# A hybrid trunk layer on one core: values between the r blocks, inverse and values in four tiles, wide triples between product bursts, and the next group's key norms and half of its sigmoids in the solve

## The chip, the core and the metric

The kernel runs on one core of a Trainium2 chip. The metric is device time in microseconds (us): the median of three runs. One more execution is profiled, and all durations of single instructions come from it. TensorE (PE) multiplies, VectorE (DVE), ScalarE (ACT) and GpSimd (POOL) work on tiles, SyncE (SP) issues transfers. Each engine works its own instructions off in the order in which the program has them and waits where an operand or a buffer isn't ready.

## The reference

One layer of a causal decoder trunk on a sequence of 1024 tokens and 1024 channels. From the normalised input, one projection gives the inputs of three branches (pooling, RWKV-7, attention to 256 memory tokens) and three gates; the branches are projected, gated and added, and a feed-forward part with a short causal convolution follows. The change lies in the RWKV-7 branch, which has 16 heads of 64 channels:

```python
zr = z_rwkv + (token_shift(z_rwkv) - z_rwkv) * mu_shift
r, k, v, dw, da, dg = jnp.split(zr, ...)
w_log = -softplus(-(w0 + tanh(dw) @ w_up_decay)) - 0.5
a = sigmoid(a0 + da @ w_up_a)
kk = k * k_k;  kk = kk * rsqrt(sum(kk * kk) + L2_EPS)      # per head: the key norm
k_eff = k * (1 + (a - 1) * k_a)
# per token t, state of 64 x 64 per head:
sa = state @ (-kk);  state = state * decay + sa (kk * a)^T + v k_eff^T;  y = state @ r
y = layer_norm(y) * ln_x_w + ln_x_b + sum(r * k_eff * r_k) * v
```

The decay is exp(-exp(w_log)), so it needs one sigmoid of w0 + ..., and a needs one of a0 + ....

## The kernel before, in words

Inputs, weights and results stay in fp32. A projection is made of *wide triples*: `mm3` (line 177) splits both factors in two fp32r parts and issues three matmuls of 128x128 by 128x512 (lines 180 to 182); each is called a wide below. Eight triples make one tile of 128 output columns by 512 tokens, so a column block has 16 triples. The two parts of a weight are made by ACT (`whi`, line 132) and POOL (`wlo`, line 139) ahead of use.

The recurrence is done in chunks of 64 tokens. `rwkv_group` (line 475) handles four groups g = 0 to 3 of four heads, as two column blocks i = 0, 1. Its parts, in program order:

- *norms and sigmoids*: `lengths` (sums of squares with the matmul `phd`, then Ln and Exp), a table load of ACT, and for each block the small matmuls `psu` (lines 502 and 503) with the sigmoids w0 (into `tBN`) and a0 (into `tHV`); the weights come by `load_up2` (line 379), which POOL splits. Then a second table load (line 208).
- *preparation* (lines 521 to 554): a scan of the decays, two Exp, the r block (48 wides, `in_block`, with a token shift on ACT, line 329, and DVE, lines 331 to 335), and copies and products that make `AR` (left factors, with r times decay at line 553) and `BK` (right factors; ACT's copies of lines 544, 549 and 550).
- *values* (lines 571 to 581): the matmul `pv` transposes v, ACT copies it to `HV`, and it is stored.
- *products* (lines 589 to 610): for each block four bursts of matmuls `ps` of 64 rows. Each burst fills two banks of four (`product_bank`), ACT copies half to `RB` and DVE multiplies half with a mask into `NT` and `AR` (lines 606 to 610). `RB` is multiplied with a mask (line 612).
- *bonus* `pbo` (line 562), after block 0, and the transposes `pt` (line 630) of `BK`.
- *solve* (lines 645 to 657): DVE inverts 32x32 triangles by forward substitution, then `place` copies the results (line 664).
- *inverse* (lines 667 to 682): `pz` and `pw` join the 32x32 parts to the inverse of 64x64 triangles, with DVE and ACT copying in between; then `NT` is stored.

A fill keeps PE at work in the solve: `group_kv` makes the next group's k and v blocks, and `fill_to(n)` (line 881) issues triples of other branches' projections until n have been issued in all: 48 more per group ahead of pz, and 256 in all ahead of the last pz. After the fourth group `chain` (line 732) runs the recurrence over the chunks, with the rest of the fill between its matmuls; its first matmul is `pr`.

`later(i, j)` only says that instruction i must stand after j, and a scheduler puts the instructions of each engine in an order that fits all of these. `PE.matmul` in fp32 shows as two records in the profile where both factors are fp32.

## Time and profile before

| what | us |
|---|---|
| median of 3 runs | 1940.28 (1934.13 to 1942.58) |
| the profiled execution | 1933.07 |
| its span | 1931.4 |
| mean granted clock of PE | 0.994 |
| DVE busy, ACT busy, POOL busy | 1366.2, 1048.7, 785.7 |

A busy time is the sum of an engine's instructions on the slowest core. In the timeline views a row has the start, the duration, the engine, the line and operation, the output and inputs with their shape, and the count of records drawn together; brackets hold the idle time ahead and what ended it. PEclk is the clock that the throttle granted to PE, as a share of full speed. The windows view gives each engine's busy time and the count of instructions in a stretch.

### The profile page before, as it was taken

What the parts mean: (1) busy time and instruction counts of PE and PEld (TensorE: products, weight loads), DVE (VectorE), ACT (ScalarE), POOL (GpSimd) and SP (SyncE); (2) the same over time, 40 slices, a digit from 0 to 9 for tenths busy, and PEclk for the clock granted to TensorE, in tenths of its full rate; (3) what the DMA queues carried; (4) which work ended last, traced back from release to release, by engine and by line L of the source; (5) the groups of instructions that cost most, each with busy time, mean ns of one, the idle gap of its engine ahead of it and who ended that gap; (6) DMA issues with size and microseconds to landing.
All of it is one profiled execution on the core that took longest, in us unless ns stands there. A gap on an engine that the chain in (4) does not pass through costs nothing.

```text
span 1931.4 us, 33821 instructions
## 1 busy us (share of the span) xinstructions
PE 1869.7 (97%) x12204; PEld 1515.9 (78%) x12204; DVE 1366.2 (71%) x2054; ACT 1048.7 (54%) x2190; POOL 785.7 (41%) x867
## 2 busy tenths in 40 slices
PE   8999999998999999999999999999999999999997
PEld 6767877876777888788788888888788888888886
DVE  8677677677677446657964534679798888877798
ACT  6685385385484355555664345555454454544544
POOL 4422221222221211121323455566599888821441
PEclk9999999999999999999999999999999999999999
DMA  5326236326239669975246444653322222289775
GB/s 165 130 73 184 93 88 179 100 77 186 94 95 303 207 195 317 329 220 183 96 139 207 130 131 141 194 164 123 105 85 90 86 80 85 88 263 211 170 189 144
DMA packets 269641, 296.28 MB, mean 153 GB/s; under 512 B 18336, under 2 KB 219168, under 8 KB 266400
## 3 DMA queue, kind: packets, MB, share of 16 engines
q1 hardware_dynamic: 248480, 271.56, 44.5%
q0 software_dynamic: 11856, 14.16, 4.5%
q10 hardware_dynamic: 9136, 8.39, 1.5%
q8 instruction: 96, 1.57, 0.3%
q14 instruction: 73, 0.60, 0.1%
HBM read 207.00 MB, written 87.03 MB: 152 GB/s over the span
## 4 chain that ended last, share of the span: by engine, by line
PE 65%; DVE 5%; DMA 3%; ACT 1%; issue 1%; POOL 0%; SPq 0%; DVEq 0%; ACTq 0%; POOLq 0%
PE psg L180 11%; PE psg L182 11%; PE psg L181 11%; PE psf L182 6%; PE psf L180 6%; PE psf L181 6%; PE psd L181 3%; PE psd L182 3%; PE psd L180 3%; PE py L780 1%; DMA R<-d_f 1%; PE pr L780 1%; PE ph L780 1%; DMA hv<-d_hv 1%; DMA gt<-d_bv 1%
## 5 line engine op out<-in xcount | busy, mean ns | idle before, releaser
L139 POOL TENSOR_TENSOR wlo<-wraw,whi 128x256 fp32r<-128x256 f32 x464 | 403.9, 883 | 827.1 <-ACT whi L132 772.8
L180 PE MATMUL psg<-hh,whi 128*128 128x512 f32 x928 | 373.9, 403 | 12.7 <-ACT whi L132 8.5
L182 PE MATMUL psg<-hh,wlo 128*128 128x512 f32 x928 | 368.7, 398 | 1.6 <-POOL wlo L139 1.4
L181 PE MATMUL psg<-hl,whi 128*128 128x512 f32 x928 | 369.0, 398 | 0.3 <-DVE hl L266 0.2
L132 ACT CAST whi<-wraw 128x256 fp32r<-128x256 f32 x472 | 181.5, 403 | 246.1 <-PE psg L181 96.1
L180 PEld LDWEIGHTS psg<-hh,whi 128*128 128x128 f32 x928 | 175.7, 189 | 55.8 <-ACT whi L132 14.4
L182 PEld LDWEIGHTS psg<-hh,wlo 128*128 128x128 f32 x928 | 176.0, 190 | 42.6 <-POOL wlo L139 4.9
L181 PEld LDWEIGHTS psg<-hl,whi 128*128 128x128 f32 x928 | 176.0, 190 | 36.7 <-issue 1.4
L1192 POOL TENSOR_TENSOR wt<-a,wt 128x256 fp32r<-128x256 f32 x136 | 155.5, 1167 | 35.3 <-ACT wt L1191 35.3
L181 PE MATMUL psd<-f,u 128*128 128x512 f32 x292 | 114.0, 390 | 0.5 <-DVE f L1608 0.4
L180 PE MATMUL psd<-f,u 128*128 128x512 f32 x292 | 113.2, 391 | 1.2 <-ACT f L1604 1.2
L182 PE MATMUL psd<-f,u 128*128 128x512 f32 x292 | 113.7, 389 | 0.0
L182 PE MATMUL psf<-h2h,wt 128*128 128x512 f32 x272 | 105.9, 389 | 0.1
L180 PE MATMUL psf<-h2h,wt 128*128 128x512 f32 x272 | 105.9, 389 | 0.0
L181 PE MATMUL psf<-h2l,wt 128*128 128x512 f32 x272 | 105.8, 389 | 0.0
L1206 DVE SCALAR_TENSOR_TENSOR d<-z,pv,d 128x1023 f32<-128x1023 f32 x68 | 101.1, 1491 | 2.1
L1192 POOL TENSOR_TENSOR wt<-s,wt 128x256 fp32r<-128x256 f32 x68 | 81.2, 1213 | 2.8 <-ACT wt L1191 1.9
L181 PE MATMUL psf<-t,wt 128*128 128x512 f32 x204 | 79.4, 389 | 0.0
L180 PE MATMUL psf<-t,wt 128*128 128x512 f32 x204 | 79.4, 389 | 0.0
L182 PE MATMUL psf<-t,wt 128*128 128x512 f32 x204 | 79.4, 389 | 0.0
L1204 ACT ACTIVATE d<-z,pv 128x1024 f32<-128x1024 f32 x34 | 42.4, 1247 | 65.7 <-DVE z L1286 49.9
L1191 ACT CAST wt<-a 128x256 fp32r<-128x256 f32 x136 | 50.7, 404 | 40.8 <-POOL wt L1192 25.9
(436 smaller groups left out, 4499.2 us busy)
## 6 DMA issues: line engine op xcount, KB each, us to landing
wraw<-in_w_in SPq DMA_DIRECT2D x176, 128.0 KB, 2.4
a<-in_w_fup SPq DMA_DIRECT2D x128, 128.0 KB, 2.4
d_ar<-AR SPq DMA_DIRECT2D x24, 512.0 KB, 4.2
d_zg<-st SPq DMA_DIRECT2D x48, 256.0 KB, 3.5
ring<-d_ar SPq DMA_DIRECT2D x8, 1536.0 KB, 11.9
wraw<-in_w_fup SPq DMA_DIRECT2D x80, 128.0 KB, 2.5
fraw<-d_f SPq DMA_DIRECT2D x33, 256.0 KB, 4.1
d_rb<-RB SPq DMA_DIRECT2D x16, 512.0 KB, 5.7
```

The source lines that it names most:

```text
L132: i = A.copy(hi, src)
L139: (V if lo_on_dve[0] else G).tensor_tensor(lo, src, hi.bitcast(F32), op=ALU.subtract)
L180: first = PE.matmul(ps, wh, xh, start=start, stop=False)
L181: PE.matmul(ps, wh, xl, start=False, stop=False)
L182: last_mm[0] = PE.matmul(ps, wl, xh, start=False, stop=stop).ins
L780: m = PE.matmul(out_, l, r, **kw)
L1191: A.copy(w[0][:, us], src[u])
L1192: low = eng.tensor_tensor(w[1][:, us], src[u], w[0][:, us].bitcast(F32), op=ALU.subtract)
L1204: A.activation(d, z, AF.Identity, scale=col("cw2", j), bias=col("cb", j))
L1206: V.scalar_tensor_tensor(d[:, n:], z[:, :T - n], col(cw, j), d[:, n:], op0=ALU.mult, op1=ALU.add)
```

## The change

- The four w0 sigmoids of a group stay in front of the preparation. The norms, the a0 sigmoids, both `load_up2` (now with a tile `ulo2` each) and the table load ahead of them are issued for group g + 1 between `group_kv` and the solve's end of group g (`lengths(g + 1, nxt)`). Group 0 has them at its start as before.
- `fill_to` ahead of pz leaves 8 triples of each group's 48 undone (`LEFT`). `covered(n)` issues n of them, behind a given instruction, at new places: 6 ahead of the w0 sigmoids, 1 between those of block 1, and in both blocks 1, 2 and 2 triples ahead of the second, third and fourth burst. In group 0 one triple goes behind the norms. In group 3 triples also go between the bonus matmuls and the first four transposes. Ahead of pz 744, 1176, 1608 and 2064 wides have been issued in all, where it was 768, 1200, 1632 and 2064.
- `values` now stands between the two r blocks, in four tiles of 64x64 at a time, two banks for each block, with both blocks in one burst of 128 records. `HV` has the memory that `NT` takes later, where it had that of `tHV`.
- pz and pw are issued for both halves in one burst each, in four tiles of 32x32, with one pair of copies ahead of pw for each half.
- The bursts of a group are put in order one behind the other (`burst`), the scan runs over 256 tokens instead of 512, and phd's two matmuls change places.

The diff, cut to its core (of what is removed, most stands in the code above and isn't repeated):

```diff
 LAST = HK - 4
+GROUP, LEFT = 48, 8
+TAKEN = 4 * GROUP + 64
 PV = {}
...
+    last_up = [None]
+    def raised(u, e, l, t0, dst, bias):
+        ps = psg.tile([P, 512], F32, name="psu", tag="g0")
+        first = PE.matmul(ps, u[0][:, e], l[:, t0:t0 + 512], start=True, stop=False)
+        last_up[0] = PE.matmul(ps, u[1][:, e], l[:, t0:t0 + 512], start=False, stop=True).ins
+        act(dst, ps, AF.Sigmoid, bias=bias)
+        return first
+    def lengths(g, kv):
         sp = rw.tile([P, 2, 2, T], FR, name="sp", tag="AR")
         tHV = rw.tile([P, 2, 2, T], F32, name="tHV", tag="HV")
+        def norms():
             for i in range(2):
                 for s, ps in square_sums(kv[i][:, 0], col("k_k", 2 * g + i), tHV[:, i, 1], sp[:, i]):
                     rstd(tHV[:, i, 1, s], ps, 1)
         if g:
-            lengths()
+            norms()
             table(SIGMOID)
+        ups = [load_up2(w_upd[2 * g + i], i) for i in range(2)]
         for i in range(2):
             for t0, _ in HALVES:
+                raised(ups[i], 1, la, t0, tHV[:, i, 0, t0:t0 + 512], col("a0", 2 * g + i))
+        return tHV, ups, norms
+    def rwkv_group(g, kv, ready):
+        tagA, tagB, tagC = ([f"X{i}{(2 * g + n) % 3}" for i in range(2)] for n in range(3))
+        tBN = [rw.tile([P, 2, T], F32, name=f"tBN{i}", tag=tagC[i]) for i in range(2)]
+        tHV, ups, norms = lengths(g, kv) if g == 0 else ready
...
+        BKs = [rw.tile([P, NCH, P], F32, name=f"BK{i}", tag=tagB[i]) for i in range(2)]
+        cover, burst = [GROUP * g - LEFT if g else 0], [None]
+        def covered(n, behind=None):
+            cover[0] += n
+            fence[0] = behind
+            wide = fill_to(cover[0])
+            fence[0] = None
+            return wide
+        if g:
+            covered(6, placed[0])
+        last = None
+        for i in range(2):
+            for t0, _ in HALVES:
+                m = raised(ups[i], 0, ld, t0, tBN[i][:, 0, t0:t0 + 512], col("w0", 2 * g + i))
+                if g and i:
+                    later(m, covered(1, last))
+                last = last_up[0]
         table(LN_EXP)
         if g == 0:
-            lengths()
+            norms()
+            covered(1)
         AR = rw.tile([P, 2, 3, T], F32, name="AR", tag="AR")
-        vs = []
+        vs = [kv[i][:, 1] for i in range(2)]
         turn = [0]
...
             return pool.tile([P, 4, 2, C], F32, name=name, tag=tag)
+        def values():
+            lo, up = slice(0, 64), slice(64, 128)
+            HV = rw.tile([P, 2, NCH, C], F32, name="HV", tag="NT")
+            after = last_mm[0]
+            for i in range(2):
+                ps = [pool.tile([P, 8, C], F32, name="pv", tag=tag)
+                      for pool, tag in (((psk, "k"), (psc, "c")) if i else ((pss, "s"), (pss, "s")))]
+                for c in range(8):
+                    for n in (1, 0):
+                        t = slice((8 * n + c) * C, (8 * n + c + 1) * C)
+                        for rows, at_ in ((lo, lo if n else up), (up, up if n else lo)):
+                            m = PE.matmul(ps[n][at_, c], vs[i][rows, t], cent[rows], start=True, stop=True)
+                            later(m, after)
+                            after = m.ins
+                for n in range(2):
+                    A.copy(HV[up, i, 8 * n:8 * n + 8], ps[n][lo if n else up])
+                    A.copy(HV[lo, i, 8 * n:8 * n + 8], ps[n][up if n else lo])
+                spill(d_hv, (g, i), HV[:, i])
+            return HV
         for i in range(2):
...
-            for t0, _ in HALVES:
-                s = slice(t0, t0 + 512)
+            for t0 in range(0, T, 256):
+                s = slice(t0, t0 + 256)
                 V.tensor_tensor_scan(t2_[:, s], smask, t2_[:, s], 0.0, op0=ALU.mult, op1=ALU.add)
             act(t3_, t2_, AF.Exp, scale=-DECAY)
             act(t2_, t2_, AF.Exp, scale=DECAY)
             V.tensor_copy(Dc[:, p], c3(t3_)[:, :, C - 1])
             in_block(8 + p, shifted(p, r_))
+            if i == 0:
+                HV = values()
             dst = c3(AR[:, i, 0])
...
             V.tensor_tensor(r_, r_, t3_, op=ALU.mult)
-            vs.append(t1_)
-
         def bonus(i):
             t0_ = kv[i][:, 0]
             for t0, _ in HALVES:
                 s = slice(t0, t0 + 512)
                 ps = pss.tile([P, 512], F32, name="pbo", tag="s")
-                PE.matmul(ps, bones, t0_[:, s], start=True, stop=True)
+                m = PE.matmul(ps, bones, t0_[:, s], start=True, stop=True)
+                if g == 3 and (i or t0):
+                    later(m, covered(1, burst[0]))
+                burst[0] = m.ins
                 V.tensor_tensor(t0_[:, s], vs[i][:, s], ps, op=ALU.mult)
...
                 ps = [product_bank("ps1"), product_bank("ps2")]
-                m = None
+                after = covered(min(2, c0 // 4), burst[0]) if c0 else None
                 for c in range(4):
                     t = slice((c0 + c) * C, (c0 + c + 1) * C)
                     for e, rows in ((1, up), (0, lo)):
+                        m = PE.matmul(ps[e][:, c], BK[i][rows, c0 + c], AR[rows, i, e:e + 2, t],
+                                      start=True, stop=True)
+                        if after is not None:
+                            later(m, after)
+                        after = m.ins
+                burst[0] = after
                 A.copy(RB[i][:, 0, cs], ps[0][:, :, 1])
...
                 for c in range(4):
-                    PE.transpose(ps[:, c], BK[i][:, c0 + c], ident)
+                    m = PE.transpose(ps[:, c], BK[i][:, c0 + c], ident)
+                    if c == i == 0 and g == 3:
+                        later(m, covered(1, burst[0]))
+                burst[0] = m.ins
                 A.copy(BKN[i][:, c0:c0 + 4], ps)
...
         nxt = group_kv(g + 1, []) if g < 3 else None
+        ready = lengths(g + 1, nxt) if g < 3 else None
         tb1 = rw.tile([P, 2, 32, 32], F32, name="tb1", tag=tagB[1])
...
         V.transpose(X.rearrange("p u t -> p t u"), S)
-        fill_to(48 * (g + 1))
+        fill_to(GROUP * (g + 1) - (LEFT if g < 3 else 0))
         if g == 3:
             w_queue[0] = A
-            fill_to(256, solve)
+            fill_to(TAKEN, solve)
         for us in (slice(0, NCH), slice(NCH, 2 * NCH)):
             for q, (qs, bs) in enumerate(quads):
                 place = V.tensor_copy(NTu[qs, us, bs], X[qs, us]).ins
+        placed[0] = place
         Z = tmp
         ends = [(slice(e, e + 32), slice(e + 32, e + 64)) for e in (0, 64)]
+        us = slice(0, 16), slice(16, 32)
+        ps = pss.tile([P, 16, 32], F32, name="pz", tag="s")
+        for u in range(16):
+            for h in range(2):
+                for ends_ in ends:
+                    m = PE.matmul(ps[ends_[1 - h], u], NTu[ends_[0], 16 * h + u, 32:64],
+                                  S11[ends_[0], 16 * h + u], start=True, stop=True)
+                    if u == h == 0:
                         later(m, place)
+        for h in range(2):
+            moved = [A.copy(Z[32:64, us[h]], ps[ends[0][1 - h]]),
+                     V.tensor_copy(Z[96:128, us[h]], ps[ends[1][1 - h]])]
+        ps = pss.tile([P, 16, 32], F32, name="pw", tag="s")
+        for u in range(16):
+            for h in range(2):
+                for ends_ in ends:
+                    m = PE.matmul(ps[ends_[h], u], Z[ends_[1], 16 * h + u],
+                                  NTu[ends_[1], 16 * h + u, 32:64], start=True, stop=True)
+                    for i in moved:
+                        later(m, i.ins)
+        for h in range(2):
+            for ends_ in ends:
+                A.copy(NTu[ends_[0], us[h], 32:64], ps[ends_[h]])
         for i in range(2):
             spill(d_nt, (g, i), NT[:, i])
-        return nxt
+        return nxt, ready
     def spill(dst, at_, src):
...
     fill += [(34 + j, spilled(d_zg[j], col("gate_b", j))) for j in range(24)]
-    filled = []
+    filled, fence = [], [None]
     def fill_steps(j, evac, behind):
...
                     later(m, behind)
+                if fence[0] is not None:
+                    later(m, fence[0])
                 filled.append(last_mm[0])
...
         return filled[n - 1]
+    placed = [None]
     first_kv = start()
     for lo in (0, 64):
         s = slice(lo, lo + 64)
         V.tensor_scalar(cent[s], ident[s, lo:lo + 64], 1.0, -1.0 / 64, op0=ALU.mult, op1=ALU.add)
     kv = group_kv(0, [first_kv])
     hi_on_act[0] = True
+    ready = None
     for g in range(4):
-        kv = rwkv_group(g, kv)
-    chain(lambda v: 279 + 121 * (v - 1) // 46 if v else 262)
+        kv, ready = rwkv_group(g, kv, ready)
+    chain(lambda v: TAKEN + 23 + (377 - TAKEN) * (v - 1) // 46 if v else TAKEN + 6)
     covered = fill_to(416)
```

What the change does to three engines, as the second group's instructions stand. First ACT, from a BK copy of the preparation on; the numbers behind the names tell tiles apart, tBN0 and BK0 are those of block 0. Before:

```order
L544 COPY BK0_2337<-BK0_2337 64x16x64
L132 CAST whi_2540<-wraw_2539 128x256
L546 ACTIVATE tHV_2336<-tHV_2336,oka_137,pv_88 128x1024
L329 ACTIVATE AR_2419<-psg_2479,omu_135 128x512
L132 CAST whi_2546<-wraw_2545 128x256
L549 COPY BK0_2337<-tBN0_2334 64x16x64
L550 COPY BK0_2337<-tBN0_2334 64x16x64
L544 COPY BK1_2338<-BK1_2338 64x16x64
L132 CAST whi_3427<-wraw_3426 128x256
L549 COPY BK1_2338<-tBN1_2335 64x16x64
L329 ACTIVATE AR_2419<-psg_2551,omu_135 128x512
L550 COPY BK1_2338<-tBN1_2335 64x16x64
```

and now:

```order
L599 COPY BK1_2377<-BK1_2377 64x16x64
L566 COPY HV_2513<-pv_2514 64x512
L567 COPY HV_2513<-pv_2514 64x512
L566 COPY HV_2513<-pv_2515 64x512
L567 COPY HV_2513<-pv_2515 64x512
L604 COPY BK0_2376<-tBN0_2374 64x16x64
L566 COPY HV_2513<-pv_2553 64x512
L567 COPY HV_2513<-pv_2553 64x512
L566 COPY HV_2513<-pv_2554 64x512
L567 COPY HV_2513<-pv_2554 64x512
L605 COPY BK0_2376<-tBN0_2374 64x16x64
L601 ACTIVATE tHV_1944<-tHV_1944,oka_137,pv_88 128x1024
```

The copies of HV, which came behind all BK copies and four casts further on, now stand between the copies of block 0's BK, and block 1's activation (line 601 now) and copies come behind them.

DVE at the end of the preparation, where the shifted r (psg), the bonus factor (kv) and r times decay (AR from AR and tBN) are made and the first evacuations (NT and AR from ps) begin. Before:

```order
L552 SCALAR_TENSOR_TENSOR kv0_1549<-AR_2419,pv_88,tHV_2336 128x1024
L553 TENSOR_TENSOR AR_2419<-AR_2419,tBN0_2334 128x1024
L331 COPY zc_2526<-psg_2551 128x1
L335 SCALAR_TENSOR_TENSOR AR_2419<-psg_2551,pv_88,AR_2419 128x511
L333 SCALAR_TENSOR_TENSOR AR_2419<-zc_2526,pv_88,AR_2419 128x1
L335 SCALAR_TENSOR_TENSOR AR_2419<-psg_2579,pv_88,AR_2419 128x511
L552 SCALAR_TENSOR_TENSOR kv1_1712<-AR_2419,pv_88,tHV_2336 128x1024
L553 TENSOR_TENSOR AR_2419<-AR_2419,tBN1_2335 128x1024
L609 TENSOR_TENSOR NT_2620<-ps2_2705,mstrict_102 64x256
L606 TENSOR_TENSOR NT_2620<-ps1_2704,mstrict_102 64x256
L607 TENSOR_TENSOR AR_2419<-ps1_2704,mstrict_102 64x256
L610 TENSOR_TENSOR AR_2419<-ps2_2705,mstrict_102 64x256
```

and now:

```order
L607 SCALAR_TENSOR_TENSOR kv0_1617<-AR_2423,pv_88,tHV_1944 128x1024
L608 TENSOR_TENSOR AR_2423<-AR_2423,tBN0_2374 128x1024
L602 TENSOR_TENSOR tHV_1944<-tHV_1944,kv1_1780 128x1024
L603 TENSOR_TENSOR tBN1_2375<-tHV_1944,tBN1_2375 128x1024
L333 COPY zc_2613<-psg_2638 128x1
L337 SCALAR_TENSOR_TENSOR AR_2423<-psg_2638,pv_88,AR_2423 128x511
L335 SCALAR_TENSOR_TENSOR AR_2423<-zc_2613,pv_88,AR_2423 128x1
L337 SCALAR_TENSOR_TENSOR AR_2423<-psg_2666,pv_88,AR_2423 128x511
L607 SCALAR_TENSOR_TENSOR kv1_1780<-AR_2423,pv_88,tHV_1944 128x1024
L653 TENSOR_TENSOR NT_2707<-ps1_2712,mstrict_102 64x256
L608 TENSOR_TENSOR AR_2423<-AR_2423,tBN1_2375 128x1024
L654 TENSOR_TENSOR AR_2423<-ps1_2712,mstrict_102 64x256
```

Block 1's last product with tBN stood ahead of all evacuations; now the first evacuation of the first burst stands ahead of it and the others behind it.

PE from the middle of the first product burst of block 0 on (line 601 before, 646 now). Before, the second burst follows the first directly:

```order
L601 MATMUL ps2_2705<-AR_2419,BK0_2337 128x128
L601 MATMUL ps1_2704<-AR_2419,BK0_2337 128x128
L601 MATMUL ps2_2705<-AR_2419,BK0_2337 128x128
L601 MATMUL ps1_2704<-AR_2419,BK0_2337 128x128
L601 MATMUL ps2_2721<-AR_2419,BK0_2337 128x128
L601 MATMUL ps1_2720<-AR_2419,BK0_2337 128x128
L601 MATMUL ps2_2721<-AR_2419,BK0_2337 128x128
L601 MATMUL ps1_2720<-AR_2419,BK0_2337 128x128
```

and now a triple stands between them:

```order
L646 MATMUL ps2_2713<-AR_2423,BK0_2376 128x128
L646 MATMUL ps1_2712<-AR_2423,BK0_2376 128x128
L182 MATMUL psg_2754<-hh_146,whi_2731 128x512
L183 MATMUL psg_2754<-hl_147,whi_2731 128x512
L184 MATMUL psg_2754<-hh_146,wlo_2732 128x512
L646 MATMUL ps2_2729<-AR_2423,BK0_2376 128x128
L646 MATMUL ps1_2728<-AR_2423,BK0_2376 128x128
L646 MATMUL ps2_2729<-AR_2423,BK0_2376 128x128
```

The third and the fourth burst have two triples ahead of them, and the scheduler adds others where they fit.

More of the change, by code (lines that the diff above doesn't have):

```diff
@@ L98, in trunk_kernel @@
     mincl = const.tile([P, 64], F32, name="mincl")
-    smask = const.tile([P, 512], F32, name="smask")
+    smask = const.tile([P, 256], F32, name="smask")
     G.memset(mstrict, 1.0)
@@ L372, in load_up, with load_up2 @@
         return hi, lo
-    ulo2 = lr.tile([P, 2, P], FR, name="ulo2")
-    G.memset(ulo2.bitcast(F32), 0.0)
-    def load_up2(ap):
+    ulo2 = [lr.tile([P, 2, P], FR, name=f"ulo2{i}") for i in range(2)]
+    for t in ulo2:
+        G.memset(t.bitcast(F32), 0.0)
+    def load_up2(ap, i):
         raw, hi, _ = up_tiles()
-        lo = ulo2
+        lo = ulo2[i]
         SP.dma_start(raw, ap)
@@ L470, in square_sums @@
             ps = pss.tile([P, 512], F32, name="phd", tag="s")
[L471 to L472 removed]
+            PE.matmul(ps, bonesr, sp[:, 1, t0:t0 + 512], start=True, stop=False)
+            PE.matmul(ps, bonesr, sp[:, 0, t0:t0 + 512], start=False, stop=True)
             yield slice(t0, t0 + 512), ps
[L475 to L476 removed]
+    last_up = [None]
[6 more added lines that the diff above has]
+    def lengths(g, kv):
         sp = rw.tile([P, 2, 2, T], FR, name="sp", tag="AR")
[L478 removed]
         tHV = rw.tile([P, 2, 2, T], F32, name="tHV", tag="HV")
[L481 to L487 removed]
+        def norms():
             for i in range(2):
@@ L570, in rwkv_group @@
         NT = rw.tile([P, 2, NCH, C], F32, name="NT", tag="NT")
-        HV = rw.tile([P, 2, NCH, C], F32, name="HV", tag="HV")
-        for i in range(2):
-            for c0 in (0, 8):
-                ps = pss.tile([P, 8, C], F32, name="pv", tag="s")
-                for c in range(8):
-                    tsl = slice((c0 + c) * C, (c0 + c + 1) * C)
-                    PE.matmul(ps[64:128, c], vs[i][0:64, tsl], cent[0:64], start=True, stop=True)
-                    PE.matmul(ps[0:64, c], vs[i][64:128, tsl], cent[64:128], start=True, stop=True)
-                A.copy(HV[64:128, i, c0:c0 + 8], ps[64:128])
-                A.copy(HV[0:64, i, c0:c0 + 8], ps[0:64])
-            spill(d_hv, (g, i), HV[:, i])
         RB = [rw.tile([P, 2, NCH, C], F32, name=f"RB{i}", tag=tagC[i]) for i in range(2)]
@@ L600, in rwkv_group @@
                     for e, rows in ((1, up), (0, lo)):
-                        m, was = PE.matmul(ps[e][:, c], BK[i][rows, c0 + c], AR[rows, i, e:e + 2, t],
-                                           start=True, stop=True), m
-                        if was is not None:
-                            later(m, was.ins)
+                        m = PE.matmul(ps[e][:, c], BK[i][rows, c0 + c], AR[rows, i, e:e + 2, t],
[4 more added lines that the diff above has]
+                burst[0] = after
                 A.copy(RB[i][:, 0, cs], ps[0][:, :, 1])
```

36 lines of the change are left out of this document (3 added, 33 removed).

## The prediction

> **What bounds the kernel now.** The page comes first: the span, and how much of it each engine works.
> ```profile
> span 1931.4 us, 33821 instructions
> PE 1869.7 (97%) x12204; PEld 1515.9 (78%) x12204; DVE 1366.2 (71%) x2054; ACT 1048.7 (54%) x2190; POOL 785.7 (41%) x867
> ```
> PE works 97% of the span, so on average only fewer or shorter PE instructions help. The change touches the four head groups alone, so I cut that stretch into stages: the timeline of PE gives the points at which each group's inverse starts and the point at which the chain begins.
> ```profile
> 372.81 1.20 PE L672 MATMUL pz<-tb,NT 32*32 32x32 f32 x64
> 373.94 0.50 PE L502 MATMUL psu<-ld,uhi 128*128 128x512 f32 x1
> 655.84 1.20 PE L672 MATMUL pz<-tb,NT 32*32 32x32 f32 x64
> 665.63 0.56 PE L780 MATMUL pr<-hv,ring 64*64 64x64 f32 x12
> ```
> The first inverse starts at 231.30 (next fence), so a period takes 141.5 us (372.81 − 231.30, and half of 655.84 − 372.81). The 9.8 us up to the first pr are the tail. Now the second group in five stages, from its predecessor's pz on: preparation, products of block 0, bonus and transposes, products of block 1, solve.
> ```profile
> core 0: us, PE busy (x) PEld busy (x) DVE busy (x) ACT busy (x) POOL busy (x), PEclk, DMA share, GB/s
> 231.30:283.70 52.40, 51.57 (x560) 40.31 (x559) 32.16 (x34) 41.34 (x62) 12.35 (x12) 1.00 0.26 78
> 283.70:291.30 7.60, 5.29 (x67) 4.27 (x67) 5.15 (x13) 7.42 (x25) 0.00 (x0) 1.00 0.61 165
> 291.30:306.00 14.70, 14.41 (x61) 9.64 (x61) 8.18 (x14) 8.21 (x15) 2.21 (x3) 1.00 0.82 242
> 306.00:319.10 13.10, 10.71 (x94) 9.06 (x93) 9.46 (x19) 10.12 (x27) 0.72 (x1) 0.87 0.40 124
> 319.10:372.80 53.70, 52.87 (x232) 42.88 (x230) 46.63 (x94) 19.08 (x40) 19.61 (x26) 1.00 0.41 124
> ```
> In the preparation PE is busy 51.57 of 52.40 us, yet ACT already has 41.34 us of work there: a preparation much shorter than that finds ACT late. In both product stages PE idles over 2 us. In the solve PE is busy 52.87 of 53.70, and DVE, which does the solve, 46.63: some 7 us of DVE slack.
>
> The two product stages on PE's timeline, with the idle time ahead of a burst and its releaser:
> ```profile
> 283.73 2.08 PE L601 MATMUL ps<-AR,BK 64*128 64x128 f32 x32
> 287.65 1.16 PE L601 MATMUL ps<-AR,BK 64*128 64x128 f32 x16 [1.41 <-DVE AR L610]
> 289.41 1.16 PE L601 MATMUL ps<-AR,BK 64*128 64x128 f32 x16 [0.60 <-DVE AR L610]
> 291.33 0.67 PE L562 MATMUL pbo<-kv,bonesr 128*128 128x512 f32 x1 [0.33 <-DVE AR L610]
> 306.02 2.06 PE L601 MATMUL ps<-AR,BK 64*128 64x128 f32 x32
> 310.77 1.16 PE L601 MATMUL ps<-AR,BK 64*128 64x128 f32 x16 [1.79 <-ACT RB L605]
> 312.53 1.99 PE L601 MATMUL ps<-AR,BK 64*128 64x128 f32 x16 [0.60 <-ACT whi L132]
> 312.00:316.00 4.00, 3.47 (x22) 3.10 (x23) 3.51 (x7) 1.71 (x6) 0.72 (x1) 0.58 0.11 33
> ```
> A burst costs 1.0 (two in 2.08). The third and fourth wait until the evacuations of an earlier burst have freed a bank: 1.41 + 0.60 + 0.33 in block 0, 1.79 + 0.60 in block 1. After the latter the granted clock falls to 0.58 for 4.00 us, a loss of 0.42 × 4.00 = 1.7.
>
> **The change part by part.** The prices, from rows: wide steps, bursts in two and four tiles, and the edge between a burst and the wides.
> ```profile
> 400.19 0.39 PE L180 MATMUL psg<-hh,whi 128*128 128x512 f32 x1
> 400.64 0.39 PE L182 MATMUL psg<-hh,wlo 128*128 128x512 f32 x1
> 245.19 0.22 PE L577 MATMUL pv<-cent,kv 64*64 64x64 f32 x1
> 245.25 0.22 PE L577 MATMUL pv<-cent,kv 64*64 64x64 f32 x1
> 245.46 0.50 PE L181 MATMUL psg<-hl,whi 128*128 128x512 f32 x1
> 245.79 0.40 PE L182 MATMUL psg<-hh,wlo 128*128 128x512 f32 x1
> 678.54 0.69 PE L780 MATMUL pu<-Rs,pair 64*64 64x64 f32 x32
> 679.16 0.50 PE L180 MATMUL psg<-hh,whi 128*128 128x512 f32 x1
> ```
> A wide in a row costs 0.227 (0.45 for two). pv, in two tiles, issues two matmuls per 0.058. The chain's pu, in four tiles, starts 32 in 0.62; as 8 × 0.058 + 0.16 that is four per 0.058 and 0.16 ahead of the burst. The first wides behind a burst take 0.33 each (245.46 to 245.79), which is 0.10 more, twice: 0.21. An edge therefore costs 0.16 + 0.21 = 0.37.
>
> *Four tiles.* pz needs 1.13 for 64 matmuls (372.81 to 373.94); four such bursts of pz and pw make 4.5 per group. All 64 pairs in four tiles go in two bursts of 1.13, so 2.2 are saved. pv has 128 matmuls, 64 × 0.058 + 4 × 0.16 = 4.4; in four tiles 32 × 0.058 + 0.16 = 2.0, so 2.4 are saved. Whether 32-row tiles overlap as pu's do isn't in the trace: the gain per group lies between 0 and 4.6, and I take 4.6 because pu's tiles also share their rows in pairs. The Trainium skill, page “TensorE: Matmul & The Clock Gate”, section “The mechanism”, says that loading weights overlaps running matmuls only where the row group differs. Two of the four new tiles have the same rows, so by that rule this term is 0; pu's four per 0.058 speak against it.
>
> *Preparation on PE.* Ahead of block 0's first product now stand 120 wides (before, 144, and the norms and eight more sigmoid matmuls): 120 × 0.227 = 27.2, pz and pw 2.3, eight sigmoid matmuls 1.8, pv 2.0, six burst edges at 0.21 1.3: 34.6 instead of 52.4. Two bursts (2.0), ten wides (2.3) and two edges (0.7) later, at 39.6, PE reaches the third burst, which needs the first one's bank.
>
> *Preparation on ACT and DVE.* This is the chain that PE now meets:
> ```profile
> 254.36 1.28 ACT L208 ACT_TABLE_LOAD   x1
> 273.83 1.05 ACT L550 COPY BK<-tBN 64x1024 f32<-64x1024 f32 x1
> 274.90 1.02 ACT L132 CAST whi<-wraw 128x256 fp32r<-128x256 f32 x3
> 276.84 0.69 ACT L329 ACTIVATE AR<-psg,omu 128x512 f32<-128x512 f32 x1 [0.91 <-PE psg L182]
> 279.80 1.70 DVE L553 TENSOR_TENSOR AR<-AR,tBN 128x1024 f32<-128x1024 f32 x1
> 281.00 0.58 ACT L579 COPY HV<-pv 64x512 f32<-64x512 f32 x1
> 285.77 0.43 DVE L609 TENSOR_TENSOR NT<-ps,mstrict 64x256 f32<-64x256 f32 x1 [4.27 <-ACT RB L608]
> ```
> pz, ten wides, three edges and pw end at about 5.8. Then ACT makes four copies of 0.58 (8.1), the four w0 sigmoids (0.69 each, as a pass of that shape), a cast (0.34) and a store copy (0.58), 11.8, and the table load, 13.1. From the table's end (255.64) to the end of the last BK copy (274.88) ACT took 19.2 before; all that work stands there again. New in this queue are the eight HV copies (8 × 0.58 = 4.7), which stood behind the BK copies; they are taken in full, since ACT idles little there. Another 1.5 (between 0 and 2 copies of 1.05) are for the second block's BK copies, which now stand behind one another. Sum 38.5. Three casts (1.0) and, from the start of the r shift to the start of AR's product, 2.96 more: 42.5. That product (1.70) now stands among the evacuations of the first burst (4 × 0.43): its bank is free at about 46.0. Then PE waits 6.4, and I price the half clock after it at 1.7, as after the 1.79 wait.
>
> pbo then starts at 46.0 + 1.0 (third burst) + 1.7 (six wides and an edge) + 1.0 (fourth) + 1.7 (half clock) = 51.4 after pz, against 60.0 (291.33 − 231.30). **Gain 8.6.**
>
> *Bonus and transposes*: two wides fewer, gain 0.4.
>
> *Products of block 1*: eleven more wides stand between the bursts, 2.5, and two more edges, 0.7. The waits of 2.4 and the half clock of 1.7 can go for it, which would gain 0.9. But DVE still needs 1.7 for each burst and multiplies RB behind them, so I leave 0.7 of wait: gain 0.2, between −1.5 (the waits only move) and 0.9. The Trainium skill, the same page, section “Why this matters for your kernels”, names idle gaps of over about 3 us between bursts as what drops the clock. By that figure the half clock behind 1.79 and 0.60 has nothing to do with these waits, its 1.7 does not go with them, and the sum would be 4 × 1.7 = 6.8 lower; the row at 0.58 stands right behind them, so I keep the credit.
>
> *Solve*: 252 wide slots instead of 230, since the norms and half of the sigmoids moved in with fewer fill triples ahead: 22 × 0.227 = 5.0, and two edges, 0.8: loss 5.8. DVE's solve would start 78 after pz and need its 46.8; PE reaches the next pz only at 138, so PE sets that end and DVE keeps over 10 us. Norms and the weights' split on ACT, DVE and POOL are hidden there (19.08 and 19.61 of 53.70 busy). If that cover were gone, they would cost no more than the two table loads of 1.28. On SP the stores of HV stand ahead of one load of a fill block and the next group's first loads; these are due over 25 us later, so I cost that at nothing (a late load would cost up to its 2 to 3 us, once per group).
>
> Net for groups 2 and 3: 8.6 + 0.4 + 0.2 − 5.8 = 3.4 each. The fourth group takes the 24 wides that the first gave up and has triples between bonus and transposes too; its solve is filled up to 256 triples in both versions: I put it at 2.6. The tail gets nine fixed wides and two bursts fewer edges: 7.2 instead of 9.8, 2.6. The first group gives up 24 wides, but they go to the fourth, and PE stands longer at its first product, with the HV copies ahead of its casts: 1.5 (between −3 and 5). **Sum 3.4 × 2 + 2.6 + 2.6 + 1.5 = 13.5.** The profiled execution (1933.07, span 1931.4) would become 1919.6. It lies at the low end of the three runs (1934.13 to 1942.58), so against their median of 1940.28 I forecast **1927**.
>
> **The rivals.** *A, PE does not wait at the third burst.* ACT's queue has idle time that takes up the HV copies, and the bank is free when PE comes. For it: ACT idles 11 of the 52.4 us. Against: most of these are ahead of the table, not behind it. Then 6.4 + 1.7 more are gained in three groups and some 3 in the first: 13.5 + 24.3 + 3 = 41, **1900**.
>
> *B, the wait is about 10 us*, because casts for the second r block also stand behind the HV copies. The gain of 3.4 vanishes in each group and what is left is the tail: **1939**.
>
> *C, four tiles do not overlap*, by the rule on row groups above. All of 4 × 4.6 = 18 goes back: 1927 + 18 = **1945**. pu's row speaks against it.
>
> *D, slower.* In block 0 the chain on ACT's queue (four HV copies ahead of each of the first block's last two BK copies) gets longer than the wides in front of PE: the casts of the r block, queued behind copies that wait for pv, hold PE up, PE delays the shift, and the shift delays the evacuations. PE then waits in two places. Each us of it costs four, one in each group. Break-even is at a wait of 6.4 + 13.5/4 = 9.8; from about 12.2 (another 9.7 in four groups) on it is slower by over 0.5%, and at 14 it would be 1940.3 − 13.5 + 4 × 7.6 = **1957**. For it: ACT is busy 41.34 of 52.40 us already, and everything gained on PE ends in this chain. Against: the waits would have to double.
>
> **How the numbers follow.** Forecast 0.52, A 0.20, B 0.10, C 0.03, D 0.15. About 0.5% (9.7 us) is what a measurement of this kernel can tell from no change. The forecast's own range, with block 1 between −1.5 and 0.9 in four groups, the first group between −3 and 5, and the wait uncertain by 2, is 1918 to 1937; some two thirds of it are faster by over 0.5%. Faster: 0.34 + 0.20 (A) = 0.54. Same: 0.18 + 0.10 + 0.03 = 0.31. Slower: 0.15 (D). From 1900 to 1948 the range holds the forecast, B, C and the nearer part of A, and leaves out D.
>
> **What would show it.** Right: the period between two pz falls by 3 to 4 us, to about 138; pbo comes 51 us after pz; the third burst of block 0 shows a wait of 4 to 8 us released by DVE's evacuation, with a granted clock below 0.7 behind it; the solve is at 59 to 60 us with PE over 97% busy; pz and pw take 1.1 each. Wrong: no wait there (A); pv or pz at the old length (C); waits ahead of casts in the r blocks, or a period over 142 (D).

## The result, and the profile after

The changed kernel takes 1959.7 us, the median of 6 runs (1955.25 to 1961.28), against 1938.09 us of the kernel before (1933.61 to 1942.58, 6 runs): a ratio of 1.0108, with a 95% interval of 1.0086 to 1.0130. It is slower by about 1.1%, where 1927 was forecast.

The page of the profile after shows nearly the same work in a longer span. PE is busy 1865.0 us instead of 1869.7; the span has grown by 22.1.

```profile
span 1953.5 us, 33838 instructions
PE 1865.0 (95%) x12204; PEld 1505.5 (77%) x12204; DVE 1358.8 (70%) x2070; ACT 1049.2 (54%) x2190; POOL 784.1 (40%) x868
```

The same five stages of the second group, as windows of the trace after (from pz: preparation, products of block 0, bonus and transposes, products of block 1, solve; the columns are those of the windows before):

```profile
239.15:274.30 35.15, 34.93 (x513) 28.10 (x513) 23.16 (x27) 30.64 (x45) 9.07 (x8) 1.00 0.41 117
274.30:291.06 16.76, 10.24 (x81) 7.98 (x81) 11.08 (x20) 10.14 (x27) 4.59 (x5) 0.80 0.24 72
291.06:305.74 14.68, 14.29 (x62) 9.52 (x60) 7.38 (x12) 7.08 (x14) 0.73 (x1) 1.00 0.72 221
305.74:318.93 13.19, 12.52 (x105) 9.70 (x105) 9.01 (x19) 11.24 (x30) 3.04 (x3) 1.00 0.46 148
318.93:387.76 68.83, 60.97 (x255) 47.67 (x254) 49.18 (x100) 27.03 (x52) 20.84 (x27) 0.95 0.31 97
```

Against before, the stages differ by −17.25, +9.16, −0.02, +0.09 and +15.13 us, which is +7.1 for the period. The first four are within 0.6 us of the forecast's −17.8, +9.2, −0.4 and −0.2. The solve was forecast at +5.8 and came out at +15.1: PE is busy only 60.97 of 68.83 us there, where before it was busy 52.87 of 53.70.

PE stands idle for 15.7 us of this period (148.61 − 132.94), and two places on its timeline hold 12.2 of them. The first is the third burst of block 0:

```profile
285.79 2.08 PE L646 MATMUL ps<-AR,BK 64*128 64x128 f32 x16 [6.52 <-DVE AR L657]
289.97 1.16 PE L646 MATMUL ps<-AR,BK 64*128 64x128 f32 x16
```

That is the wait of 6.4 that the forecast had. The second, in the solve, was in no part of it; PE is on the small matmuls of the moved a0 sigmoids:

```profile
356.76 0.47 PE L483 MATMUL psu<-la,uhi 128*128 128x512 f32 x1 [0.62 <-ACT tHV L216]
...
358.47 0.40 PE L183 MATMUL psg<-hl,whi 128*128 128x512 f32 x1
364.57 0.80 PE L483 MATMUL psu<-la,uhi 128*128 128x512 f32 x1 [5.71 <-DVE kv L337]
365.16 0.63 PE L484 MATMUL psu<-la,ulo 128*128 128x512 f32 x1
```

PE stands 5.71 us for DVE's shift of the v block (line 337 now). DVE's timeline of the same moment shows where that shift was queued:

```profile
360.06 2.02 DVE L707 STREAM_TRANSPOSE tb<-tb 128x1024 f32<-128x1024 f32 x1
361.97 1.89 DVE L708 STREAM_TRANSPOSE tb<-tb 128x1024 f32<-128x1024 f32 x1
363.70 0.17 DVE L335 SCALAR_TENSOR_TENSOR kv<-zc,pv,kv 128x1 f32<-128x1 f32 x1
363.77 0.75 DVE L337 SCALAR_TENSOR_TENSOR kv<-psg,pv,kv 128x511 f32<-128x511 f32 x1
```

It stands behind the last two transposes of the solve. `raised` takes its banks from tag g0 (two banks, taken in turn), which the next group's k and v blocks use too, and the shift is the last reader of the bank that the second pair of a0 matmuls gets. Before the change nobody asked for these banks until pz was done, so a late shift would have cost nothing; it was not late either, since DVE's order had it ahead of both transposes (rows of the kernel before):

```profile
355.55 0.74 DVE L335 SCALAR_TENSOR_TENSOR kv<-psg,pv,kv 128x511 f32<-128x511 f32 x1
360.66 2.24 DVE L656 STREAM_TRANSPOSE tb<-tb 128x1024 f32<-128x1024 f32 x1
```

So two things came with the change: PE asks for the bank within the solve, and DVE empties it later. The clock falls as well, around and behind the wait:

```profile
359.00:364.50 5.50, 0.00 (x0) 0.00 (x0) 5.33 (x10) 3.53 (x5) 0.00 (x0) 0.66 0.00 0
364.00:372.00 8.00, 7.43 (x27) 6.08 (x28) 6.46 (x13) 2.00 (x4) 0.00 (x0) 0.77 0.02 9
```

At 0.77 for 8.00 us the second window loses 0.23 × 8.00 = 1.8. The waits view of PE says that this happens in other groups too (total us, times, longest); in the solves of the first three groups the second pair of a0 matmuls waits 4.61, 5.71 and 5.73:

```profile
PE ps L646 <- DVE AR L657: 21.1, 5, 6.5
PE psu L483 <- DVE kv L337: 16.7, 4, 5.7
```

### The profile page after: what moved, and what is told of

It reads as the page before. It is cut to its first block, busy times and chain, and to the rows that moved or that the text cites. A ratio compares the mean times of both kernels' runs of the same rounds, so it can differ in the third digit from the quotient of the medians.

```text
span 1953.5 us, 33838 instructions
## 1 busy us (share of the span) xinstructions
PE 1865.0 (95%) x12204; PEld 1505.5 (77%) x12204; DVE 1358.8 (70%) x2070; ACT 1049.2 (54%) x2190; POOL 784.1 (40%) x868
## 4 chain that ended last, share of the span: by engine, by line
PE 76%; DVE 12%; DMA 4%; ACT 4%; issue 3%; POOL 1%; SPq 0%; ACTq 0%; POOLq 0%; DVEq 0%
PE psg L182 14%; PE psg L184 14%; PE psg L183 14%; PE psf L184 5%; PE psf L182 5%; PE psf L183 5%; PE psd L183 3%; PE psd L184 3%; PE psd L182 3%; DVE tb L706 2%; DVE tb L704 2%; PE py L839 2%; DMA wraw<-in_w_in 1%; DMA Q<-in_w_fdn 1%; PE pr L839 1%
## 5 line engine op out<-in xcount | busy, mean ns | idle before, releaser
L182 PE MATMUL psg<-hh,whi 128*128 128x512 f32 x928 | 381.3, 411 | 15.0 <-ACT whi L134 9.9
```

What stands on the lines that cost most here:

```text
L182: first = PE.matmul(ps, wh, xh, start=start, stop=False)
```

## The experiments

Theory T: the solve got longer because of that bank, behind DVE's solve. Rival D, from the prediction: the waits at the third burst, behind the HV copies on ACT, made the kernel slower. Rival M: norms and sigmoids cost PE too much in the solve as such. Each median is told with its ratio to the kernel before on the same chip and its 95% interval. Where runs come from different chips the ratios compare better than the medians: the kernel before took 1938.09 with the result and 1935.33 with e1 to e4.

| run | median us | ratio to before |
|---|---|---|
| e1_own_bank | 1934.16 | 0.9995 (0.9983 to 1.0007) |
| e2_shift_earlier | 1934.67 | 1.0001 (0.9986 to 1.0015) |
| e3_values_behind | 1957.84 | 1.0114 (1.0094 to 1.0135) |
| e4_norms_back | 1948.49 | 1.0074 (1.0059 to 1.0089) |
| e5_shift_on_act | 1934.20 | 0.9982 (0.9968 to 0.9995) |
| e6_late_products | 1928.77 | 0.9959 (0.9945 to 0.9974) |
| e7_both | 1933.05 | 0.9983 (0.9974 to 0.9992) |
| e8_pv_two_tiles | 1935.98 | 0.9998 (0.9982 to 1.0014) |
| e9_casts_behind | 1929.48 | 0.9968 (0.9957 to 0.9979) |
| e10_casts_pv_two | 1932.46 | 0.9985 (0.9976 to 0.9994) |
| f1_best | 1921.70 | 0.9923 (0.9908 to 0.9938) |
| f2_no_cover | 1932.01 | 0.9982 (0.9969 to 0.9995) |

### e1: other banks for the a0 sigmoids

```diff
+        pool, tag = bank or (psg, "g0")
-        ps = psg.tile([P, 512], F32, name="psu", tag="g0")
+        ps = pool.tile([P, 512], F32, name="psu", tag=tag)
...
-                raised(ups[i], 1, la, t0, tHV[:, i, 0, t0:t0 + 512], col("a0", 2 * g + i))
+                raised(ups[i], 1, la, t0, tHV[:, i, 0, t0:t0 + 512], col("a0", 2 * g + i),
+                       ((psk, "k"), (psc, "c"))[t0 // 512] if g else None)
```

> The changed kernel, with the a0 sigmoids' matmuls of the solve written to two banks that the product bursts use (free in the solve) instead of bank g0, whose last user is the next group's v block. Theory T (the solve got longer because PE waits there for DVE to empty bank g0, behind the end of DVE's solve): the waits of 5.7 us in three solves go, with the lower clock behind them, so 3 times 7 to 9 us: about 1935 (1932 to 1939), periods of about 140. Rival D (the waits ahead of the third burst, behind the HV copies on ACT, made it slower): these waits stay, so no change, 1955 to 1960. Rival M (norms and sigmoids cost PE as much in the solve as wides do, and 252 slots are too many): no change either.

Measured 1934.16, in T's range. By the medians that is 25.5 us less than the changed kernel, by the ratios (1.0108 and 0.9995) about 22. On PE's timeline the a0 matmuls follow without a wait; the solve (a window of the second group, as above) takes 61.25 us instead of 68.83, at full clock:

```profile
349.91 0.39 PE L484 MATMUL psu<-la,uhi 128*128 128x512 f32 x1
...
351.44 0.40 PE L485 MATMUL psu<-la,ulo 128*128 128x512 f32 x1
```

```profile
312.23:373.48 61.25, 59.52 (x255) 46.43 (x254) 52.16 (x100) 26.77 (x52) 21.17 (x27) 1.00 0.36 109
```

Rivals D and M, which expected no change, fall: the waits at the third burst are still there (6.5 us) and the norms are still in the solve.

### e2: the same bank, the shift earlier on DVE

```diff
+            if s == 25 and g < 3:
+                later(m_, last_shift[0])
```

(`m_` is the product of step s of the solve, `last_shift` the last shift of the v block.)

> The changed kernel with one order edge more: DVE's last shift of the next group's v block stands ahead of the 26th step of the solve, not behind its last transposes. Bank g0 stays the one that the a0 matmuls use. T: the shift runs some 6 to 8 us earlier, bank g0 is free when PE comes, and the gain is nearly that of the run with other banks: 1933 to 1943; a DVE wait of 1 to 3 us appears in the solve and costs nothing. If it is the bank's other readers and not the place in DVE's queue, no change: 1955 to 1960. D: no change.

Measured 1934.67. Bank g0 is kept, and one order edge on another engine gives the same gain. On DVE's timeline the shift comes between two steps of the solve, in PE's order the a0 matmuls follow (the first waits 0.62, the second not at all):

```profile
348.97 0.75 DVE L337 SCALAR_TENSOR_TENSOR kv<-psg,pv,kv 128x511 f32<-128x511 f32 x1
349.63 0.31 DVE L704 TENSOR_TENSOR tb<-tb 128x156 f32<-128x156 f32 x1
```

```profile
349.08 0.47 PE L483 MATMUL psu<-la,uhi 128*128 128x512 f32 x1 [0.62 <-DVE kv L337]
...
350.78 0.39 PE L483 MATMUL psu<-la,uhi 128*128 128x512 f32 x1
```

So it was the place in DVE's queue, and the bank only passed it on to PE. T stands, shown from two sides.

### e3: the values behind both r blocks

```diff
-            if i == 0:
-                HV = values()
...
-            HV = rw.tile([P, 2, NCH, C], F32, name="HV", tag="NT")
+            HV = rw.tile([P, 2, NCH, C], F32, name="HV", tag="HV")
...
+        HV = values()
         NT = rw.tile([P, 2, NCH, C], F32, name="NT", tag="NT")
```

> The changed kernel with the values (four tiles) behind both r blocks again and HV in the memory that tHV had. D: the HV copies leave ACT's queue ahead of the BK copies, the wait of 6.5 ahead of the third burst shrinks by 4 us or more in each group and the kernel gains 10 us or more: 1940 to 1950. T: the waits in the solve stay; the copies now hold the four banks ahead of the first burst, so the product stage waits there instead: 1950 to 1962.

Measured 1957.84, no gain, as T had it. The HV copies left the preparation's queue, and the third burst no longer waits; but PE now waits for them at the first burst, since they hold the banks:

```profile
275.95 2.10 PE L562 MATMUL pv<-cent,kv 64*64 64x64 f32 x128
282.81 0.79 PE L645 MATMUL ps<-AR,BK 64*128 64x128 f32 x2 [4.76 <-ACT HV L567]
```

D's remedy only moves its wait. Where the change put the values is no worse than the old place.

### e4: norms and sigmoids back at the group's start

```diff
-        tHV, ups, norms = lengths(g, kv) if g == 0 else ready
+        tHV, ups, norms = lengths(g, kv)
...
-        ready = lengths(g + 1, nxt) if g < 3 else None
+        ready = None
```

> The changed kernel with norms, all sigmoids and the up loads of a group at its start again, as before the change. T: the waits in the solve go (9 us per group with the clock), but ACT starts its chain about 8 us later against 5 us more of PE work, so the wait ahead of the third burst grows to 9 to 12 us: 1938 to 1950. If having the norms in the solve is worth its price apart from the bank, this run is slower than the run with other banks by 5 us or more. D: the same 1955 to 1965 or slower.

Measured 1948.49, within T's 1938 to 1950, and slower than e1 by 14 us: away from the bank, moving the norms was worth that. The wait did not grow at the third burst as expected (6.3 us); it came up front, for ACT's sigmoids:

```profile
241.49 0.79 PE L483 MATMUL psu<-la,uhi 128*128 128x512 f32 x1 [4.29 <-ACT tHV L216]
```

The total was expected, the place was not.

### e5 and e6: the queues ahead of the third burst

With the bank mended the kernel is where it was before the change (0.9995). Theory W says why the four tiles and the shorter preparation bring nothing: what PE saves it waits for at the third burst, behind ACT and DVE. e5 has block 1's last two BK copies behind the scaling of r, e6 has two long DVE products of block 1 behind the second evacuation.

```diff
+            last_scale[0] = A.activation(d, ps, AF.Identity, scale=omu[:, m:m + 1]).ins
...
+            for m in (A.copy(BK[0:64, :, 64:128], c3(t2_)[0:64]),
+                      A.copy(BK[64:128, :, 0:64], c3(t2_)[64:128])):
+                if i:
+                    later(m, last_scale[0])
```

> The run with own banks (1934), with one edge on ACT: block 1's two last BK copies stand behind the scaling of the second half of block 1's r (line 331), which they preceded. Theory W (the wait of 6.5 us ahead of the third burst is the queue on ACT and DVE in front of the first evacuations, and the gain of the change went into it): the scaling runs 3 us earlier, DVE's idle time of 3.3 us ahead of the shift goes, the wait falls to about 3.3: 3 groups times 3 to 5.5 us, 1918 to 1926. If the wait is the bursts' own evacuations, no change: 1932 to 1937.

Measured 1934.20: a miss, the wait is still 6.5. The reason stands on ACT's timeline, one row ahead of the scaling: a cast of weights in the same queue, whose load has not come, holds it by 4.23 us.

```profile
270.89 0.40 ACT L134 CAST whi<-wraw 128x256 fp32r<-128x256 f32 x1 [4.23 <-DMA wraw<-in_w_in]
271.20 0.68 ACT L331 ACTIVATE AR<-psg,omu 128x512 f32<-128x512 f32 x1
```

In e1 that cast stood behind the BK copies and its load had time to land. The edge took away the cover of a second wait.

```diff
-            V.scalar_tensor_tensor(t0_, r_, col("r_k", p), t4_, op0=ALU.mult, op1=ALU.mult)
-            V.tensor_tensor(r_, r_, t3_, op=ALU.mult)
+            def rest(t0_=t0_, r_=r_, p=p, t4_=t4_, t3_=t3_):
+                for m in (V.scalar_tensor_tensor(t0_, r_, col("r_k", p), t4_, op0=ALU.mult, op1=ALU.mult),
+                          V.tensor_tensor(r_, r_, t3_, op=ALU.mult)):
+                    if evac[0] is not None:
+                        later(m, evac[0])
+            if i == 0:
+                rest()
...
+                if i == 0 and c0 == 4:
+                    rest()
```

> The run with own banks (1934), with block 1's bonus factor and its product with the decay (1.28 and 1.21 us on DVE) behind the evacuations of the second burst of block 0. W: the third burst waits about 4.0 instead of 6.5: 3 groups times 2.5 to 4.8 us, 1920 to 1928. If the wait is set by ACT alone, no change.

Measured 1928.77, just short of the range. The third burst waits 2.0 us less:

```profile
274.96 2.08 PE L653 MATMUL ps<-AR,BK 64*128 64x128 f32 x16 [4.51 <-DVE AR L664]
```

Part of W is shown: DVE's queue is in that wait.

### e7: both

> Both edits, on the run with own banks. W: the wait ahead of the third burst falls to about 1 us and the lower clock behind it goes too: 3 groups times 5.5 to 8 us, 1910 to 1918, faster than the kernel before by about 1%. If something else stands behind the wait (PE itself is late, or the fourth burst then waits), 1920 or more.

Measured 1933.05, no better than e1 within the intervals' width and worse than e6 alone. The same cast holds ACT (4.06 us in this run), and the third burst waits 5.4. On SP's queue one sees the load behind it:

```profile
264.29 0.36 SPq L764 DMA_DIRECT2D d_hv<-HV  x1
268.48 5.65 SPq L170 DMA_DIRECT2D wraw<-in_w_in  x5
```

The store of HV, which waits for ACT's copies, stands ahead of the load, but it is issued 4.2 us before it, so it is not the only candidate: the load also needs a buffer that POOL frees after an earlier cast. Which of the two holds the load back was not tried apart.

### e8: pv in two tiles, with the wait still there

```diff
-                for c in range(8):
-                    for n in (1, 0):
+                for n in (1, 0):
+                    for c in range(8):
```

> The run with own banks (1934), with pv in two tiles at a time (2.0 us more of PE per group, the order of its matmuls is all that changes). W: pv stands in front of the third burst's wait, which shrinks by as much; no change, 1932 to 1937, and the wait is 4.5. If PE work counts in full, 4 times 2.0: 1942.

Measured 1935.98, no change (0.9998 against 0.9995). pv takes 3.43 us instead of 2.09, and the third burst waits 4.97 instead of 6.52:

```profile
254.37 3.43 PE L564 MATMUL pv<-cent,kv 64*64 64x64 f32 x128
```

```profile
278.82 1.96 PE L648 MATMUL ps<-AR,BK 64*128 64x128 f32 x16 [4.97 <-DVE AR L659]
```

What PE loses ahead of a wait, the wait gives back, and the other way round: as long as that wait stands, the four tiles of pv save PE's time and nothing of the kernel's.

### e9 and e10: the casts behind the scaling, and pv in two tiles again

```diff
+            if g and i == 0:
+                hold[0] = scaled_r[0]
             in_block(16 + p, shifted(8 + p, t[:, 0]))
+            if g and i == 0:
+                hold[0] = None
```

(`hold` puts the casts of this k block behind the given instruction, here the scaling of block 1's r in the group ahead.)

> The run with both edits (1933), with the four casts of the next group's first k block behind the scaling of r on ACT as well; in that run the last of them waited 4.06 us for its weights in front of the scaling, and the third burst still waited 5.4. W: the scaling starts when PE has finished r, the third burst's wait falls to 0.5 to 2 us and the lower clock behind it goes: 3 groups times 4 to 7 us, 1912 to 1921. If the casts come too late for the k block, PE waits for them in the bonus stage and the gain is less: 1921 to 1930. If the weights' load was not the cause, no change: 1931 to 1935.

Measured 1929.48. In the second and third group W is right: the third burst waits 1.56 instead of 6.52, and their periods are 137.5 and 137.6, where e1 had 141.6 and 142.3. But a new wait of 2.50 stands at the bonus, the first group is 2.7 us longer, and the fourth, which has no next k block to hold, still waits 5.5. The total falls short of W's range. It lies in the range of the second expectation, but not for its reason: the wait at the bonus is for DVE's evacuation, not for the casts.

```profile
275.97 1.16 PE L660 MATMUL ps<-AR,BK 64*128 64x128 f32 x16 [1.56 <-DVE AR L671]
...
282.30 1.10 PE L629 MATMUL pbo<-kv,bonesr 128*128 128x512 f32 x2 [2.50 <-DVE AR L671]
```

> The run before with pv in two tiles at a time. W: with the wait gone, PE's 2.0 us per group count where they were hidden before: 4 to 8 us slower than the run it is made from. If they are hidden by something else too, the same within 2 us.

Measured 1932.46, 3.0 us slower than e9: between the two expectations. The 1.56 left of the wait still hid most of the 1.34 that pv costs per group; the third burst waited 0.26 there. So most of the 3.0 is not pv in these groups; in the profiled runs 1.3 of it lies in the first group, whose pz comes at 235.87 instead of 234.59, and the rest is not traced.

### f1: the best version, and f2: no triples between the bursts

f1 is e9 with the two products of block 1 behind all four bursts' evacuations (`c0 == 12` for `c0 == 4`), and with the edges on ACT in the second and third group alone.

> Made from the run with casts behind: block 1's bonus factor and product with the decay now stand behind the evacuations of all four bursts of block 0 (there, DVE's 1.27 and 1.23 held up the bonus matmuls by 2.50), and the edges on ACT are kept in the second and third group only, since the first and the last were slower with them. W: the wait of 2.5 ahead of the bonus goes in three groups and the first group is back at 137 to 138: 1916 to 1924. If the bonus then waits for the same work elsewhere, 1925 to 1930.

Measured 1921.70, in W's range and 0.8% faster than the kernel before. The second group's stages in it:

```profile
230.37:265.50 35.13, 34.90 (x514) 28.10 (x513) 23.13 (x27) 30.64 (x44) 9.04 (x8) 1.00 0.42 118
265.50:276.93 11.43, 8.58 (x81) 6.53 (x80) 8.40 (x18) 9.18 (x26) 3.01 (x4) 1.00 0.12 35
276.93:294.21 17.28, 15.84 (x68) 10.81 (x68) 9.72 (x14) 8.09 (x17) 2.21 (x3) 1.00 0.82 242
294.21:307.40 13.19, 12.52 (x106) 9.69 (x105) 9.01 (x19) 11.33 (x30) 3.05 (x3) 1.00 0.46 148
307.40:366.34 58.94, 57.69 (x249) 45.37 (x246) 51.21 (x100) 26.08 (x51) 20.33 (x26) 1.00 0.37 111
```

The period is 136.0, with full clock throughout. The preparation is that of the changed kernel to 0.02 us; what made the difference are the two queues behind it. The reason that was expected holds only in part, though. The bonus of the second group still waits twice for DVE (1.29 and 1.10, in e9 2.50 and 0.86), and in the fourth group it waits 3.31. Of the gain on e9, 4.2 us lie in the first group (its pz comes at 230.37 instead of 234.59), where the products moved and the edges on ACT are gone; the two were not run apart.

f2 is e1 without `covered` between the bursts of the first three groups:

```diff
-                after = covered(min(2, c0 // 4), burst[0]) if c0 else None
+                after = (covered(min(2, c0 // 4), burst[0]) if g == 3 else burst[0]) if c0 else None
```

> The run with own banks (1934) without the triples between the product bursts of the first three groups (they are issued in the solve; the last group keeps them). If these triples are what fills waits there, block 1's waits of 2.4 and the half clock of 1.7 come back in three groups, while block 0 keeps its end: 1938 to 1946. If PE's waits are set by DVE in any case and the triples only move, no change: 1932 to 1937.

Measured 1932.01, no change from e1 (0.9982 against 0.9995, the intervals overlap). Waits as before the change are back in block 1 (1.64 and 0.60 in the second group), and block 0 keeps its wait of 5.43; against that the bursts stand in pairs and have fewer edges. The triples between bursts, as they stand, are worth nothing that these runs show.

## Why the prediction was wrong, point by point

**The sign and the size.** 1927 was forecast with 0.15 for slower; it became 1959.7, beyond the range of 1900 to 1948.

**The step that failed** is the solve: “Norms and weights' split on ACT, DVE and POOL are hidden there”, and with it the solve's loss of 5.8 and the bound that a lost cover costs no more than two table loads of 1.28. I asked whether ACT, DVE and POOL had time for the moved work, and they had. I didn't ask who owned the bank that the moved matmuls write, and where its last reader stands in its own engine's queue. The forecast had DVE's solve end at 78 + 46.8 = 124.8 after pz, and so it did (the shift behind it starts at 363.77 − 239.15 = 124.6). But it compared this with the pz at 138, while the second pair of a0 matmuls asked for its bank at 364.57 − 5.71 − 239.15 = 119.7. The moved a0 matmuls wait for bank g0, and through it for DVE's solve. e1 and e2 show it: by the ratios about 22 us, the whole loss against the kernel before. In the profiled runs the solve of the first three groups, from the end of the last transpose to pz, goes from 67.7, 68.6 and 69.2 to 59.6, 61.0 and 61.0 us with other banks.

**The rivals.** D's time, 1957, is close to the measured one by luck, since D's mechanism is not what happened: the third burst waited 6.52, not 14, and no cast in the r blocks held up PE in groups 2 to 4. e3 shows that taking D's cause away gains nothing. A (no wait) is refuted by the row of the third burst, and so is B (10 us). B's 1939 did not follow from its own words either: with nothing left but the tail's 2.6 it would have been 1937.7. C is refuted by the bursts in four tiles: 128 matmuls of pz with 1.22 us from the first to the next wide, and 128 of pv in 2.02.

```profile
261.17 2.09 PE L562 MATMUL pv<-cent,kv 64*64 64x64 f32 x128
263.19 0.50 PE L182 MATMUL psg<-hh,whi 128*128 128x512 f32 x1
```

**What was right.** The preparation on PE, 34.6 forecast, 35.15 measured. The chain on ACT and DVE: 46.0 and a wait of 6.4 forecast; the third burst started at 285.79 − 239.15 = 46.64, after 6.52 of wait. The bonus at 51.4 forecast, 51.91 measured. The tail at 7.2, measured 7.32. The Trainium skill, page “TensorE: Matmul & The Clock Gate”, section “The mechanism”, has weight loads overlap running matmuls only where the row group differs. As the prediction read that, the four tiles would have been no faster; the rows above disagree, and the measurement decides.

**Sizes that were off even with the bank mended.** e1's period in the second group is 141.59, where 138.1 was forecast: preparation 0.5 more than forecast, products of block 0 0.5, bonus 0.4, block 1 0.3, solve 1.7 (0.9 of it is more idle time of PE, 1.73 against 0.83; the rest is open). An edge was priced at 0.37 with 0.10 more on two wides. In the changed kernel only the first wide behind a burst takes 0.33 (306.83 to 307.17), the second 0.23, and a burst with one triple takes 1.99 (305.74 to 307.73), so an edge came to 1.99 − 1.0 − 3 × 0.227 = 0.3. Each of these sizes is small, and together they are about the 3.4 that the forecast had as gain. In the fourth group I wrote “I put it at 2.6” without working it out: 24 more wides in it are 24 × 0.227 = 5.4, and the period came out 1.9 us longer, not 2.6 shorter. In the first group a gain of 1.5 was forecast; with the bank mended it ends at 231.89 in e1's profile and at 231.06 in e2's, before the change at 231.30, so no gain shows.

**Why the change brings nothing without the bank's wait.** In e1's second group PE's busy time is only 2.9 us shorter than before, since most of what left the preparation stands in the solve and between the bursts now, and its idle time is 3.0 us longer (6.64 before, 9.61 in e1). The whole period in one window, before and in e1 (there as the sum of the five stages):

```profile
231.30:372.81 141.51, 134.87 (x1009) 106.15 (x1009) 101.58 (x172) 86.18 (x165) 34.88 (x42) 0.99 0.41 121
sum 141.59, PE 131.98 PEld 102.00 DVE 102.72 ACT 85.92 POOL 38.59; mean PE 26.40 PEld 20.40 DVE 20.54 ACT 17.18 POOL 7.72
```

PE's savings lie ahead of the third burst, which is set by ACT and DVE. e8 shows it for pv; e6, e9 and f1 give the savings back by shortening those two queues, and f1 stands 14.0 us below the kernel before on its chip (1921.70 against 1935.74). That this is close to the 13.5 that I had forecast for the change alone is luck: f1 has other banks and shorter queues besides, and its third burst waits 1.56, not 6.4.

## What to carry to other kernels

When a step moves into another stage, ask for every buffer that it takes who frees it there, and where that reader stands in its own engine's queue; idle time of the engines doesn't answer this. Work saved ahead of a wait is worth nothing until the chain that ends the wait is shorter too: find the instructions in front of the releaser and order them first. And when an edge in a queue brings nothing, look one row ahead of the instruction that was moved, since another wait may have been hidden under the one you took away.

## What the runs showed of the hardware

The granted clock does not follow one wait alone. In the kernel before, block 1 has waits of 1.79 and 0.60 in the second group and the third alike, and the windows around them differ:

```profile
309.00:317.00 8.00, 5.63 (x42) 4.87 (x43) 7.35 (x17) 5.55 (x18) 0.72 (x1) 0.79 0.21 68
451.00:459.00 8.00, 5.01 (x48) 4.09 (x48) 7.25 (x17) 6.15 (x20) 0.73 (x1) 1.00 0.22 72
```

So the 1.7 that I credited for the end of those waits was not due in every group. In e9 a wait of 2.50 went by at a granted clock of 1.00, while each of the waits of 4.3 us and more that the text shows was followed by rows at half speed (matmul steps of 0.43 instead of 0.23 us behind 285.79 in the changed kernel). The rule of the Trainium skill, page “TensorE: Matmul & The Clock Gate”, section “Why this matters for your kernels”, which names gaps over about 3 us, fits these longer waits; the half clock behind 1.79 and 0.60 it does not explain.
